# Triangular products of eight chunks in one run instead of two runs of four, in a decoder trunk with three token mixers

## The chip, the cores and the metric

The kernel runs on one core of a Trainium2 chip. The metric is the device time of one execution in microseconds; before the change its median over three runs is 2262.69 us (2262.41 to 2262.93).

The names of the engines in the profile: PE is TensorE (matmuls), PEld its weight loads, DVE is VectorE, ACT is ScalarE, POOL is GpSimd, and SP is SyncE, which issues the transfers.

## The reference, cut to what matters

The reference is a trunk of two layers over 1024 tokens of width 1024. Each layer takes an RMSNorm with a conditioned shift and scale, one wide input projection, three causal token mixers (pooling, retention, RWKV-7), a projection of each, gates, an output projection and the residual. The change lies in the RWKV-7 mixer, which has 8 heads of 64 channels and for each token:

```
def step(S, inp):
    r_t, w_t, k_t, v_t, a_t, b_t = inp
    sa = jnp.einsum('bhvk,bhk->bhv', S, a_t)
    S = (S * w_t[:, :, None, :] + sa[..., None] * b_t[:, :, None, :]
         + v_t[..., None] * k_t[:, :, None, :])
    return S, jnp.einsum('bhvk,bhk->bhv', S, r_t)
```

The kernel does this in 16 chunks of 64 tokens. Inside a chunk the recurrence turns into triangular matrices: products of the decayed keys and removal vectors (b, k) with the decayed receptances and key directions (r, a), of which a mask keeps the causal part. These are the triangular products.

## The kernel before, in words

Activations lie with channels on the 128 partitions and tokens along the free dimension, in two halves of 512. Nearly all of TensorE's time goes into dense projections: 128x512 products, three for each tile of weights, since weights and activations are split into a high and a low part (acc in the profile).

The RWKV mixer runs over four pairs of heads in each of two layers (rwkv_task, L1296). For one pair: prepare(h) makes from k, r and v of half h the tiles AR and BK (both operands of the triangular products, 8 chunks to a half). scores(h) (L1402) follows: two times four transposes of BK (tile bt), then the triangular products, then a masking multiplication on VectorE that moves them from PSUM to the tile G, then bonus(h), a sum over a head by two products (tile bon). scores(0) runs side by side with prepare(1); scores(1) follows. After that come the value products (states, L1474, tile av), the inversion of the triangular matrices (invert, on VectorE in the double bank), the block products (blocks, L1493, 32x32), and the state loop over 16 chunks (L1527).

One triangular product multiplies 64 partitions (one head) by 128 columns on each side. The two heads of a pair lie on partitions 0 to 63 and 64 to 127, so the kernel issues them by turns, and the two run side by side on TensorE's two row halves. Each takes two matmul instructions in float32.

PSUM is split up so: three banks for the dense projections (psa, tag acc), two rotating banks shared by all small work (psm, function mx, L609: transposes, norms, scores, value products, retention, pooling), one double bank held for the whole kernel as a single tile "two" of 2 x 512 columns, of which cyt() (L619) hands out the halves by turns, and one bank "ch" (psc), which the state loop uses for the values inside a chunk and the state update (L1547). The lead-in uses "two" and "ch" too. In the triangular products before the change, head 0 writes a rotating bank and head 1 a half of "two".

The order of the work is set in two steps. First the program is recorded: nothing is issued, each operation goes into a list, with a clock of its own that decides which task comes next (a generator's yield is the time after which it wants to go on). Second, a planner (plan, L341) replays the list with estimated durations: at each step it takes the engine that is free first and, among its ready operations, the one with the smallest key; the key is the place in the list, and the RWKV lane gets 3000 places of advantage (BIAS, L121). An operation that needs a new tile waits until its tag has a free slot. "with nc.together()" (L270) makes several matmuls one operation, which is never broken up. Two rules of the planner touch the change: entering the 64-row form is priced at 250 ns and leaving at 200 (ENTER and LEAVE, L117), and an operation of 16 or more matmuls waits for up to four dense products since the last such one (SPELL, L476):

```
if len(o.calls) >= 16 and spell < SPELL:
    rest = [x for x in now if x.big]
    if rest:
        o = min(rest, key=lambda o: o.key)
```

All instructions are issued from one place, so every row of the profile has the line L548, and rows are told apart by their tiles.

Of the kernel before, what the change touches and what calls it, by code (L numbers as in the profile page):

```python
# [9 lines left out]
F32 = mybir.dt.float32  # L10
# [3 lines left out]
ALU = mybir.AluOpType  # L14
# [3 lines left out]
P = 128  # L18
# [4 lines left out]
HF = 512  # L23
# [538 lines left out]
def trunk_kernel(ctx, tc, xT, cvec, pos, vecs, consts, w_ada, w_all, pool_w, lora_w, out):  # L562
    nc = Log(tc.nc, tc)

    def pool(name, bufs, **kw):
        return PoolProxy(nc, ctx.enter_context(tc.tile_pool(name=name, bufs=bufs, **kw)), bufs, "")
# [12 lines left out]
    ps_c = pool("psc", 1, space=PSUM)  # L579
# [9 lines left out]
    def nm(s):  # L589
        uid[0] += 1  # L590
        return f"{s}_{uid[0]}"
# [17 lines left out]
    def mx(s):  # L609
        t = ps_m.tile([P, HF], F32, tag="mx", name=nm(s))  # L610
        if len(mxq) == 2:
            behind[t.name] = mxq.popleft()
        mxq.append(t.name)
        return t
# [4 lines left out]
    def cyt():  # L619
        turn[0] ^= 1  # L620
        return two[:, turn[0] * HF : (turn[0] + 1) * HF]
# [4 lines left out]
    def r8(s):  # L626
        return rp.tile([P, 2048], F32, tag="r8", name=nm(s))

    o = CST["bone"]
# [8 lines left out]
    def cs(k, n=None):  # L638
        o = CST[k]
        return cst[:, o : o + n] if n else cst[:, o : o + 1]  # L640
# [165 lines left out]
    hd = [dp.tile([8, 2, P, HF], F32, name=f"hd{l}") for l in range(L)]  # L806
# [28 lines left out]
    def settle():  # L835
        if seen[0] is None:
            return
        for j in range(seen[0], len(nc.ops)):
            o = nc.ops[j]
            e, ins, outs = o.eng, o.ins_, o.outs  # L840
            t = max([ready.get(x.tensor.name, 0.0) for x in ins] + [0.0])
            base = t if any(x.space == PSUM for x in ins) else clock[0]
            if e == "PE":
                t = clock[0] + 280
            elif e != "SP":
                c = cost(o)
                idle_at[e] = max(idle_at[e], base) + c
                t = max(t + c, idle_at[e]) + 80
                for x in ins:
                    if x.space == PSUM:  # L850
                        ready[x.tensor.name] = max(ready.get(x.tensor.name, 0.0), t)
            for x in outs:
                ready[x.tensor.name] = t
        seen[0] = len(nc.ops)

    def await_(out, *ins):
        names = [x.tensor.name for x in ins] + [behind.pop(out.tensor.name, "")]
        clock[0] = max(clock[0], *(ready.get(n, 0.0) for n in names))
# [16 lines left out]
    def wait(*aps, spare=0.0):  # L875
        settle()
        names = [x.tensor.name if hasattr(x, "tensor") else x.name for x in aps]
        t = max(ready.get(n, 0.0) for n in names) + spare
        if len(mxq) == 2:
            t = max(t, ready.get(mxq[0], 0.0) + 600)  # L880
        return max(0.0, t - clock[0])
# [8 lines left out]
    def until(t):  # L890
        return max(0.0, t - clock[0])
# [51 lines left out]
    def mmul(out, lhsT, rhs, start=True, stop=True, timed=False, **kw):  # L943
        n = rhs.free_size()
        fast = rhs.dtype == F32R
        settle()
        await_(out, *(() if timed else (lhsT, rhs)))
        m = lhsT.free_size()
        clock[0] += (n + 32) / 2.4 if fast else 2 * max(n, 1.6 * m - 92, m - 16) * 0.875
        return nc.tensor.matmul(out, lhsT=lhsT, rhs=rhs, start=start, stop=stop, **kw)  # L950

    def trans(out, in_, timed=False):
        settle()
        await_(out, *(() if timed else (in_,)))
        clock[0] += 109.0
        nc.tensor.transpose(out, in_, ident)
# [339 lines left out]
    def rwkv_task(l, hp, kT, rT, vp, lt):  # L1296
        lw = lora_load(l, hp)
        AR = r8("AR").rearrange("p (c j t) -> p c j t", j=2, t=CH)
        BK = r8("BK").rearrange("p (c j t) -> p c j t", j=2, t=CH)
        Gf = gtile("G")  # L1300
        G = Gf[:, 0 : 32 * P].rearrange("p (u n) -> p u n", n=P)
# [6 lines left out]
        rm = cs("rmask", P).unsqueeze(1).to_broadcast([P, 4, P])  # L1308
        jt = lambda t, rows, c: t[rows, c, :, :].rearrange("p j t -> p (j t)")
# [81 lines left out]
        def bonus(h):  # L1391
            yield wait(*rks[h], spare=500)
            ps = mx("bon")
            mmul(ps, bone, rks[h][0], start=True, stop=False)
            mmul(ps, bone, rks[h][1], start=False, stop=True)
            bv = t_ri("bv")
            nc.vector.scalar_tensor_tensor(bv, ps, 0.5, vp[h], op0=ALU.mult, op1=ALU.mult)
            bvs.append(bv)
# [3 lines left out]
        def scores(h):  # L1402
            yield max(until(whole[h] + 1000), wait(Z, spare=600))
            for q in range(2):
                ps = mx("bt")
                c0 = 8 * h + 4 * q
                n = min(4, 15 - c0)
                with nc.together():
                    for c in range(n):
                        trans(ps[:, c * P : (c + 1) * P], jt(BK, slice(0, P), c0 + c), timed=True)  # L1410
                nc.scalar.copy(BKt[:, c0 : c0 + n, :], ps[:, 0 : n * P].rearrange("p (c n) -> p c n", n=P))
                yield 1300
            for q in range(2):
                c0 = 8 * h + 4 * q
                gps = [mx("g"), cyt()]
                with nc.together():
                    for j in range(4):
                        for hd in range(2):
                            rows = slice(64 * hd, 64 * hd + 64)
                            mmul(gps[hd][:, j * P : (j + 1) * P], jt(BK, rows, c0 + j), jt(AR, rows, c0 + j), timed=True)  # L1420
                for hd in range(2):
                    u0 = 16 * hd + c0
                    nc.vector.tensor_tensor(
                        G[:, u0 : u0 + 4, :], gps[hd].rearrange("p (u n) -> p u n", n=P), rm, op=ALU.mult
                    )
                yield 2600
            yield from bonus(h)
        yield from prepare(0)
        yield from side(scores(0), prepare(1))
        nc.gpsimd.memset(Z[0:64, :, :], 0.0)  # L1430
        yield from scores(1)
        prog[(l, hp)] = 0
        MT = r8("MT")
# [93 lines left out]
        for c in range(16):  # L1527
# [19 lines left out]
            ch = ps_c.tile([P, HF], F32, tag="ch", name=nm("ch"))  # L1547
            for hd in range(2):
                cols = slice(64 * hd, 64 * hd + 64)
                u0 = (16 * hd + c) * P  # L1550
                n = 65
# [24 lines left out]
            o = (c % 8) // 2 * P  # L1576
            yout.append(nc.scalar.copy(y[64 * par : 64 * par + 64, o : o + P], cy[0:64, 0:P]).ins)
            yield wait(Sn)
            if c % 8 == 7:
                h = c // 8  # L1580
# [370 lines left out]
    for l in range(L):  # L1951
# [200 lines left out]
        for p, (ia, ib) in enumerate(pairs):  # L2152
# [9 lines left out]
            for it in (ia, ib):  # L2162
                for h in range(2 if it[0] == "wg" else 0):
                    o = (t_vp if h else t_cs)("wo")
# [51 lines left out]
        while wready[0][0][0] != "out":  # L2216
# [6 lines left out]
            elif it[0] == "gate":  # L2223
                n, d = it[1], it[2]
# [3 lines left out]
            else:  # L2228
                n, d0 = it[1], it[2]
# [3 lines left out]
                for d, h in [(d, h) for h in range(2) for d in (d0, d0 + 1)]:  # L2233
# [5 lines left out]
                    o = (d % 2) * T + h * HF  # L2239
# [182 lines left out]
```

## Time and profile before

| | |
|---|---|
| median of three runs | 2262.69 us (2262.41 to 2262.93) |
| the profiled execution | 2262.4 us |
| its span | 2260.6 us |
| TensorE's granted clock, mean | 0.997 |
| triangular products, matmul instructions into the rotating bank / the double bank | 256 / 256 |
| masking multiplications on VectorE | 64, some 0.68 us each |

The page of the profile gives busy times of the engines, the span in 40 slices, the chain of work that ended last, and groups of instructions. Further views answer for a part: groups by line and tile, the timeline (instructions in order, with "xN" for N merged ones, and in brackets the idle time before one with what ended it), and busy time by stretches. Of the names in the rows, g is the rotating bank's tile of triangular products, two is the double bank, ch the bank of the intra-chunk values, acc a dense projection, and G the masked result. Ends of matmuls are modelled, since they are pipelined; the distance between two starts is the better measure.

### The profile page before, as it was taken

How to read it: one execution, taken by the hardware profiler on the slowest of the kernel's cores; microseconds unless marked ns; L12 is line 12 of the kernel's file. 1: busy time of each engine (PE TensorE's matmuls, PEld its weight loads, DVE VectorE, ACT ScalarE, POOL GpSimd, SP SyncE). 2: the span in 40 equal slices, each digit the busy share in tenths (PEclk: the TensorE clock that was granted, in tenths of full speed). 3: DMA queues.
4: the chain of work that ended last, by engine and by line, in shares of the span. 5: the costliest groups of instructions: out<-in, count | busy, mean ns of one | idle time of the engine just before them, and what ended most of it. 6: DMA issues, size and time to landing. Idle time of an engine off the chain costs nothing.

```text
span 2260.6 us, 34881 instructions
## 1 busy us (share of the span) xinstructions
PE 2229.0 (99%) x12980; PEld 1865.3 (83%) x12980; DVE 1589.5 (70%) x2750; ACT 931.5 (41%) x1795; POOL 627.0 (28%) x564
## 2 busy tenths in 40 slices
PE   7999999999999999999999999999999999999998
PEld 6788888888888888888878888888888888888888
DVE  7996877958878765668667678587686744465854
ACT  5634434434344344323454343353443444442243
POOL 2223323323325233332122132333332500041311
PEclk9999999999999999999999999999999999999999
DMA  8222111112236664654541111111122533256442
GB/s 318 70 59 72 34 43 42 51 46 70 86 119 218 200 201 130 229 187 167 172 134 31 45 41 44 55 38 49 40 82 93 182 112 112 89 184 218 135 131 85
DMA packets 138906, 249.36 MB, mean 110 GB/s; under 512 B 15728, under 2 KB 20080, under 8 KB 138736
## 3 DMA queue, kind: packets, MB, share of 16 engines
q1 hardware_dynamic: 138736, 247.14, 34.1%
q8 instruction: 102, 1.67, 0.3%
q14 instruction: 68, 0.56, 0.1%
HBM read 187.57 MB, written 59.51 MB: 109 GB/s over the span
## 4 chain that ended last, share of the span: by engine, by line
PE 89%; DVE 7%; ACT 2%; issue 1%; DMA 1%; SPq 0%; DVEq 0%; ACTq 0%
PE acc L548 73%; PE two L548 3%; PE ch L548 2%; PE ro L548 1%; PE g L548 1%; PE av L548 1%; DVE two L548 1%; DVE tm L548 1%; DVE ksq L548 1%; PE rs L548 1%; DVE G L548 1%; PE rkv L548 1%; PE m L548 1%; PE bt L548 1%; PE lw L548 1%
## 5 line engine op out<-in xcount | busy, mean ns | idle before, releaser
L548 PE MATMUL acc<-hhi,wh 128*128 128x512 f32 x1488 | 597.1, 401 | 1.6 <-DVE vp L548 1.1
L548 PE MATMUL acc<-hhi,wl 128*128 128x512 f32 x1488 | 596.9, 401 | 0.0
L548 PE MATMUL acc<-hlo,wh 128*128 128x512 f32 x1488 | 596.3, 401 | 0.0
L548 POOL TENSOR_TENSOR wl<-wr,wh 128x512 fp32r<-128x512 f32 x171 | 228.4, 1335 | 585.8 <-ACT wh L548 440.5
L548 PEld LDWEIGHTS acc<-hhi,wh 128*128 128x128 f32 x1488 | 280.5, 189 | 50.8 <-DVE vp L548 1.5
L548 PEld LDWEIGHTS acc<-hhi,wl 128*128 128x128 f32 x1488 | 280.6, 189 | 48.7
L548 PEld LDWEIGHTS acc<-hlo,wh 128*128 128x128 f32 x1488 | 280.6, 189 | 47.3
L548 ACT CAST wh<-wr 128x512 fp32r<-128x512 f32 x242 | 149.3, 617 | 268.3 <-PE acc L548 215.5
L548 PE MATMUL acc<-T,wh 128*128 128x512 f32 x576 | 177.6, 389 | 0.0
L548 PEld LDWEIGHTS acc<-T,wh 128*128 128x128 f32 x576 | 108.1, 188 | 22.4
L548 DVE SCALAR_TENSOR_TENSOR S<-ch,pc,SP 64x64 f32<-64x64 f32 x224 | 63.3, 283 | 87.1 <-PE ch L548 84.3
L548 PE MATMUL acc<-T,wl 128*128 128x512 f32 x288 | 112.1, 389 | 0.0
L548 DVE TENSOR_TENSOR wl<-wsum,wh 128x512 fp32r<-128x512 f32 x63 | 45.3, 719 | 78.7 <-ACT wh L548 78.4
L548 ACT CAST wh<-wsum 128x512 fp32r<-128x512 f32 x96 | 59.5, 620 | 96.6 <-PE acc L548 92.9
L548 ACT COPY Z<-ch 64x128 f32<-64x128 f32 x128 | 33.0, 258 | 132.6 <-PE ch L548 132.0
L548 POOL TENSOR_TENSOR oz<-ol,oz 128x512 fp32r<-128x512 f32 x10 | 14.0, 1401 | 264.8 <-DVE wl L548 179.7
L548 DVE TENSOR_TENSOR tm<-MT,two 64x30 f32<-64x30 f32 (+14 forms) x240 | 76.3, 318 | 11.4 <-ACT two L548 4.6
L548 DVE TENSOR_TENSOR two<-two,tm 64x30 f32<-64x30 f32 (+14 forms) x240 | 78.9, 329 | 7.1
L548 PE MATMUL acc<-oy,wh 128*128 128x512 f32 x256 | 80.1, 394 | 0.0
L548 PE MATMUL acc<-oG,wh 128*128 128x512 f32 x256 | 79.0, 390 | 0.0
L548 PE MATMUL acc<-oz,wh 128*128 128x512 f32 x256 | 78.9, 389 | 0.0
L548 DVE TENSOR_TENSOR wl<-wraw,wh 128x512 fp32r<-128x512 f32 x48 | 33.7, 703 | 63.5 <-ACT wh L548 63.5
(332 smaller groups left out, 4863.5 us busy)
## 6 DMA issues: line engine op xcount, KB each, us to landing
wr<-in_w_all SPq DMA_DIRECT2D x268, 256.0 KB, 2.7
wraw<-in_w_all SPq DMA_DIRECT2D x96, 256.0 KB, 2.7
gd<-gsg SPq DMA_DIRECT2D x96, 256.0 KB, 2.0
gs<-gd SPq DMA_DIRECT2D x96, 256.0 KB, 3.8
wada<-in_w_ada SPq DMA_DIRECT2D x80, 256.0 KB, 2.9
ol<-od SPq DMA_DIRECT2D x48, 256.0 KB, 3.5
traw<-hd SPq DMA_DIRECT2D x32, 256.0 KB, 3.0
x<-in_xT SPq DMA_DIRECT2D x16, 256.0 KB, 5.2
```

The lines of the kernel that those rows point to most:

```text
L548: o.inst = f(*a, **k)
```

## The change

The two runs of four chunks become one run of eight. The first four chunks write a rotating bank (head 0) and one half of the double bank (head 1), as before. The other four write the bank "ch" and the other half of the double bank, where before they took a second rotating bank and the other half of the double bank. All 16 products are one operation of the planner. The four masking multiplications follow, two and two, with the same yields.

```
-            for q in range(2):
-                c0 = 8 * h + 4 * q
-                gps = [mx("g"), cyt()]
-                with nc.together():
-                    for j in range(4):
-                        for hd in range(2):
-                            rows = slice(64 * hd, 64 * hd + 64)
-                            mmul(gps[hd][:, j * P : (j + 1) * P], jt(BK, rows, c0 + j), jt(AR, rows, c0 + j), timed=True)
+            gps = [mx("g"), cyt(), ps_c.tile([P, HF], F32, tag="ch", name=nm("ch")), cyt()]
+            with nc.together():
+                for j in range(8):
+                    for hd in range(2):
+                        rows = slice(64 * hd, 64 * hd + 64)
+                        o = j % 4 * P
+                        mmul(
+                            gps[j // 4 * 2 + hd][:, o : o + P], jt(BK, rows, 8 * h + j), jt(AR, rows, 8 * h + j), timed=True
+                        )
+            for q in range(2):
                 for hd in range(2):
-                    u0 = 16 * hd + c0
+                    u0 = 16 * hd + 8 * h + 4 * q
                     nc.vector.tensor_tensor(
-                        G[:, u0 : u0 + 4, :], gps[hd].rearrange("p (u n) -> p u n", n=P), rm, op=ALU.mult
+                        G[:, u0 : u0 + 4, :], gps[2 * q + hd].rearrange("p (u n) -> p u n", n=P), rm, op=ALU.mult
                     )
                 yield 2600
```

## The prediction

> **What bounds the kernel now.** I read the page first, from the top: the span, the busy times, and the chain that ended last.
>
> ```profile
> span 2260.6 us, 34881 instructions
> PE 2229.0 (99%) x12980; PEld 1865.3 (83%) x12980; DVE 1589.5 (70%) x2750; ACT 931.5 (41%) x1795; POOL 627.0 (28%) x564
> PE 89%; DVE 7%; ACT 2%; issue 1%; DMA 1%; SPq 0%; DVEq 0%; ACTq 0%
> ```
>
> PE is busy for all but 31.6 us of the span, and the chain runs along PE for 89% of it. So latency on another engine is worth nothing by itself here: what counts is PE time that does no work. A busy share cannot show that, because overlapping matmuls count as busy even where their starts lie too far apart. I therefore went to the runs of the triangular products and read the distance between starts.
>
> Second view: busy time by stretch of the matmuls that write the rotating bank (tile g), one stretch around each of the 16 calls of scores. There is one call for each half of the sequence, eight pairs of heads in all. Four of the 16 rows and the sum; behind the stretch and its length stands PE's busy time with the count of instructions:
>
> ```profile
> 102.00:108.00 6.00, 2.31 (x16) 1.00 0.00 0
> 121.00:127.00 6.00, 2.40 (x16) 1.00 0.22 82
> 275.00:281.00 6.00, 2.05 (x16) 1.00 0.17 47
> 1659.00:1665.00 6.00, 2.05 (x16) 1.00 0.27 85
> sum 96.00, PE 35.71; mean PE 2.23
> ```
>
> Every stretch has the same 16 instructions, yet some need 2.05 us and others 2.31 or more. The 2.05 us rows are those in which the planner already puts the two runs of four chunks directly behind each other. There are seven of them (the first is at 275, the last at 1659), all in the second call for a head pair. The other nine are still split: all eight first calls, and the second call at 121. **So the change can only join nine runs, not sixteen.**
>
> **The change part by part. (a) One entry into and one exit from the 64-row form saved, nine times.** The timeline of PE around the split pair at 121, and around the joined pair at 275 (start, duration, engine, line, operation, output and inputs, shapes, count):
>
> ```profile
> 121.39 0.40 PE L548 MATMUL acc<-hlo,wh 128*128 128x512 f32 x1
> 121.72 0.37 PE L548 MATMUL g<-AR,BK 64*128 64x128 f32 x1
> ...
> 122.81 0.51 PE L548 MATMUL acc<-hhi,wl 128*128 128x512 f32 x1
> 123.15 0.40 PE L548 MATMUL acc<-hhi,wh 128*128 128x512 f32 x1
> 123.39 0.40 PE L548 MATMUL acc<-hlo,wh 128*128 128x512 f32 x1
> 123.62 0.40 PE L548 MATMUL acc<-hhi,wl 128*128 128x512 f32 x1
> 123.94 0.49 PE L548 MATMUL g<-AR,BK 64*128 64x128 f32 x2
> 124.25 0.37 PE L548 MATMUL two<-AR,BK 64*128 64x128 f32 x1
> ```
>
> ```profile
> 275.78 0.40 PE L548 MATMUL acc<-hhi,wh 128*128 128x512 f32 x1
> 276.10 0.37 PE L548 MATMUL g<-AR,BK 64*128 64x128 f32 x1
> ...
> 278.09 0.51 PE L548 MATMUL acc<-hlo,wh 128*128 128x512 f32 x1
> 278.43 0.40 PE L548 MATMUL bon<-rkh,bone 128*128 128x512 f32 x1
> ```
>
> Dense products follow each other every 0.23 us (123.15, 123.39, 123.62). I count from the last dense start before a run to the second full-width start after it and take off two such slots. The run of four chunks costs 123.15 - 121.39 - 0.46 = 1.30 us. Eight chunks joined cost 278.43 - 275.78 - 0.46 = 2.19 us. Two separate runs cost 2.60 us, so a join saves 0.41 us of PE.
>
> Five of the nine second runs are followed by the transposes of v, where leaving the form is cheaper:
>
> ```profile
> 1351.02 0.39 PE L548 MATMUL acc<-hlo,wh 128*128 128x512 f32 x1
> 1352.43 0.33 PE L548 MATMUL vt<-cst,vp 128*128 128x128 f32 x1
> 1352.60 0.38 PE L548 MATMUL vt<-cst,vp 128*128 128x128 f32 x2
> ```
>
> Here it is 1352.60 - 1351.02 = 1.58 us, less a dense slot of 0.23 and one transpose at its pace of 0.11 (the two merged into the last row take 0.38 together, one alone 0.27). That makes 1.24 us for the second run. Joined, the second half costs 2.19 - 1.30 = 0.89, so 0.35 us are saved. Sum of (a): 4 x 0.41 + 5 x 0.35 = **3.4 us**.
>
> The Trainium skill, TensorEngine Tiling (Array Packing), Key Properties, states that changing the tiling mode drains TensorE. Its page TensorE: Matmul & The Clock Gate, Single matmul latency, gives a fixed part of about 166 ns warm for a matmul that cannot hide its drain. Estimated from that page, two changes of mode cost 0.33 us and nine joins 3.0 us; the rows say 0.35 to 0.41, so the mechanism agrees and the size is nearly its own.
>
> **(b) The wait inside the second run goes.** In the row at 123.94 the second run starts, but its first product for the other head, into the double bank, starts 0.31 us later, at 124.25. Through that time PE is held: the queue is in order. On VectorE, and at the last split:
>
> ```profile
> 123.52 0.68 DVE L548 TENSOR_TENSOR G<-two,cst 128x512 f32<-128x512 f32 x1
> 1644.99 0.48 PE L548 MATMUL g<-AR,BK 64*128 64x128 f32 x2
> 1645.31 0.37 PE L548 MATMUL two<-AR,BK 64*128 64x128 f32 x1
> ```
>
> The first run's double-bank half is read until 123.52 + 0.68 = 124.20, and the held matmul starts 0.05 us behind that, although it writes the other half. The double bank is one tile, and the wait is set for the whole of it. Seven of the nine second runs are held so, by 0.09 to 0.42 us (0.31 at 124.25, 0.32 at 1645.31, the last), together **1.8 us**. In the joined run all products are issued before any of its own evictions, so nothing holds them: the run at 276.10 shows none of it.
>
> **(c) One rotating-bank tile fewer per call.** The second quarter of the products goes to the intra-chunk bank instead. After the joined pair at 276:
>
> ```profile
> 277.30 0.69 DVE L548 TENSOR_TENSOR G<-g,cst 128x512 f32<-128x512 f32 x1 [1.85 <-PE g L548]
> 278.84 0.68 DVE L548 TENSOR_TENSOR G<-g,cst 128x512 f32<-128x512 f32 x1
> 279.44 0.68 DVE L548 TENSOR_TENSOR G<-two,cst 128x512 f32<-128x512 f32 x1
> 279.13 0.39 PE L548 MATMUL acc<-hhi,wh 128*128 128x512 f32 x1
> 279.67 0.72 PE L548 MATMUL av<-Z,G 128*65 128x64 f32 x9
> ```
>
> The value products (av) start 0.54 us behind a dense product instead of 0.23, right behind the eviction that ends at 279.52. They write the rotating bank that this eviction frees, not what it produces: their chunks belong to the first call. That is 0.31 us, in four of the eight pairs (279.67 the first, the others at 1368, 1515 and 1663). With the new layout only the first eviction frees a rotating bank, which was done at 277.99, 1.5 us earlier, and the other bank is free from the start. So I take 4 x 0.31 = **1.2 us**. Nothing back would be the lower end.
>
> **(d) What is added.** The run now needs the intra-chunk bank and both halves of the double bank at once. Both were last used by the state loop of the head pair before:
>
> ```profile
> 386.87 0.40 PE L548 MATMUL ch<-xst,G 128*65 128x64 f32 x4
> 403.52 0.37 PE L548 MATMUL g<-AR,BK 64*128 64x128 f32 x1
> ```
>
> That loop ends 16 us before the next run (this is the narrowest of the seven), so no wait: zero. The planner lets an operation of 16 or more products wait until four dense ones have passed since the last such operation. The only ones before are the block products, which lie ahead of the state loop that has just been shown to be over; so this is zero too. The four evictions of one call stay four; their order on VectorE is free to change.
>
> Sum: 3.4 + 1.8 + 1.2 = 6.4 us. The profiled execution took 2262.4 us (span 2260.6), so 2256.0 for it. The median of the runs is 2262.69, 0.3 us above it, which gives **2256.3 us**. The time cannot be sharper than the planner: it fits the whole order anew around the change, and the stalls that its estimates miss move by up to about 2 us either way (all of PE's idle time together is 31.6 us).
>
> **The rivals.** *Banks and evictions give it back.* The four evictions follow a run at 0.60 us each (278.84, 279.44), 2.4 us, while the run itself takes 1.8 us. If VectorE now sets the pace, the next user of a rotating bank waits in place of the second run. In the first calls that would be the transposes of v, and the av wait stays. At the av price of 0.31 us that is 8 x 0.31 = 2.5 us lost and 1.2 not gained: 6.4 - 3.7 = 2.7 us faster, 2260.0 us. For it: VectorE is 70% busy and in these stages more. Against: the merged run fills its first bank halfway, so that bank is emptied while PE goes on (277.30, with the run lasting to 278.09). The Trainium skill, TensorEngine Tiling (Array Packing), PSUM Bottleneck, warns of just this, that packing speeds up TensorE but not the emptying of PSUM; the seven joined runs of this trace show it in the av wait alone.
>
> *Slower: the chain behind a first call becomes late.* With the run of eight chunks ahead of the norm products of the other half, those come 0.89 us later. If all four evictions also go ahead of them on VectorE, two more evictions of 0.60 us lie in the way: 2.1 us per head pair, 16.8 us over eight. Net it would be 6.4 - 16.8 = 10.4 us slower, 2273.1 us. It decides only where PE has no dense product left to fill with. Against it:
>
> ```profile
> 405.00:552.00 147.00, 146.92 (x1015) 123.02 (x1014) 109.99 (x220) 61.45 (x130) 45.88 (x46) 1.00 0.16 52
> ```
>
> From 405 to 552, a whole head pair, PE idles 0.08 us. The chain has cover, and the second evictions are recorded 2600 ns of the planner's clock behind the first, so they need not go ahead.
>
> *The change does less than it says*, in that the planner has joined most runs already: that is no rival but a row, and stands in the sum (nine, not sixteen). It cannot do nothing, since one grouped operation cannot be split.
>
> **How the numbers follow.** The forecast case (a + b and most of c) has 0.68. Its own range is 2253.5 to 2258.2: the sum less or plus the 2 to 3 us by which the order can shift. The case in which banks and evictions give it back has 0.26 and runs from 2258.2 to 2262.7. The late chain has 0.06. The range of 8 in 10 reaches from 2253.5 to 2261.0. It leaves out the late chain, the last part of the second case and a little below. No change is 0.2% here, 4.5 us, about what a measurement of this kernel can tell; so faster means below 2258.2. Faster 0.68, same 0.26, slower 0.06.
>
> **What would show it.** In the new profile: sixteen runs of 32 matmul instructions, none of 16; g tile stretches with half the instructions each; no start of a double-bank product more than 0.02 us behind its partner's; av directly on a dense product's 0.23 us slot; PE busy time down by about what the span loses. It is wrong if transposes of v or bonus products start more than 0.5 us behind a dense product, if the intra-chunk bank turns up as a reason for waiting, or if PE idles in the state loops.

## The result, and the profile after

The changed kernel takes 2255.75 us (median of six runs, 2254.5 to 2260.26) against 2262.83 us for the kernel before in the same measurement: a ratio of 0.9968 with a 95% interval of 0.9955 to 0.9981, 7.1 us faster. A second measurement on another occasion gave 2255.98 against 2261.82 us, 0.9976 (0.9967 to 0.9985). The forecast was 2256.3.

The page of the profiled execution (2256.61 us):

```profile
span 2254.8 us, 34865 instructions
PE 2224.4 (99%) x12980; PEld 1865.8 (83%) x12980; DVE 1590.2 (71%) x2753; ACT 931.2 (41%) x1795; POOL 628.3 (28%) x561
PE 90%; DVE 6%; ACT 2%; issue 1%; DMA 0%; POOL 0%; SPq 0%; DVEq 0%; POOLq 0%; ACTq 0%
```

The same 12980 matmul instructions are there, PE is busy for 4.6 us less, and the span is 5.8 us shorter. This execution had a slower start: the first triangular run begins at 104.36 us instead of 103.08, with the same order of PE's work up to there. From that point to the end (2260.6 - 103.1 against 2254.8 - 104.4) the change gained 7.1 us.

Busy time by stretch, here of the matmuls into the double bank (tile two), one stretch around each of the 16 calls; two of the rows and the sum:

```profile
102.00:108.00 6.00, 2.05 (x16) 1.00 0.00 0
121.00:127.00 6.00, 2.05 (x16) 1.00 0.28 89
sum 96.00, PE 32.77; mean PE 2.05
```

All sixteen calls now need 2.05 us; none is split. The timeline of PE around the call that was split at 121, here from 122:

```profile
122.67 0.40 PE L548 MATMUL acc<-hlo,wh 128*128 128x512 f32 x1
123.00 0.37 PE L548 MATMUL g<-AR,BK 64*128 64x128 f32 x1
123.00 0.37 PE L548 MATMUL two<-AR,BK 64*128 64x128 f32 x1
...
124.98 0.51 PE L548 MATMUL acc<-hhi,wl 128*128 128x512 f32 x1
125.32 0.40 PE L548 MATMUL acc<-hhi,wh 128*128 128x512 f32 x1
```

From the dense start at 122.67 to the second one behind the run, at 125.32, it is 2.65 us, as long as the joined run of before. The first product into the double bank starts with its partner (123.00 and 123.00), not 0.31 us behind. And VectorE and PE behind the second call of the second head pair:

```profile
275.62 0.69 DVE L548 TENSOR_TENSOR G<-g,cst 128x512 f32<-128x512 f32 x1 [1.47 <-PE g L548]
276.53 0.69 DVE L548 TENSOR_TENSOR G<-two,cst 128x512 f32<-128x512 f32 x1 [0.22 <-PE two L548]
277.14 0.68 DVE L548 TENSOR_TENSOR G<-ch,cst 128x512 f32<-128x512 f32 x1
277.74 0.68 DVE L548 TENSOR_TENSOR G<-two,cst 128x512 f32<-128x512 f32 x1
```

```profile
277.22 0.39 PE L548 MATMUL acc<-hlo,wh 128*128 128x512 f32 x1
277.45 1.10 PE L548 MATMUL av<-Z,G 128*65 128x64 f32 x16
```

The value products start 0.23 us behind a dense start, while the eviction of the intra-chunk bank is still going on. The wait of 0.31 us is gone.

### The profile page after: what moved, and what is told of

Read it like the earlier page. It is cut to its first block, busy times and chain, and to the rows that moved or that the text cites. A ratio compares the mean times of both kernels' runs of the same rounds, so it can differ in the third digit from the quotient of the medians.

```text
span 2254.8 us, 34865 instructions
## 1 busy us (share of the span) xinstructions
PE 2224.4 (99%) x12980; PEld 1865.8 (83%) x12980; DVE 1590.2 (71%) x2753; ACT 931.2 (41%) x1795; POOL 628.3 (28%) x561
## 4 chain that ended last, share of the span: by engine, by line
PE 90%; DVE 6%; ACT 2%; issue 1%; DMA 0%; POOL 0%; SPq 0%; DVEq 0%; POOLq 0%; ACTq 0%
PE acc L548 74%; PE two L548 3%; PE ch L548 3%; PE av L548 1%; PE ro L548 1%; DVE two L548 1%; DVE tm L548 1%; PE g L548 1%; PE rs L548 1%; DVE ksq L548 1%; PE bt L548 1%; PE lw L548 1%; PE rkv L548 1%; DVE G L548 0%; PE m L548 0%
## 5 line engine op out<-in xcount | busy, mean ns | idle before, releaser
L548 DVE TENSOR_TENSOR tm<-MT,two 64x30 f32<-64x30 f32 (+14 forms) x240 | 76.3, 318 | 13.1 <-ACT two L548 6.3
L548 ACT COPY y<-two 64x128 f32<-64x128 f32 x128 | 33.1, 258 | 108.5 <-PE two L548 106.9
```

The source lines that it names most:

```text
L548: o.inst = f(*a, **k)
```

## The experiments

The kernels were measured in several groups, on different chips, each together with the kernel before, whose median was 2261.82 to 2262.83 us. The ratios are to the kernel before in the same group; differences of times across groups are uncertain by about 1 us.

To compare the profiled executions I add up by how much the starts of PE's instructions lie further apart than at the usual pace (228 ns for a dense product of 512 columns, 110 for 128 columns, 56 for an instruction of a triangular product). There are three sums. *Cost of the 64-row form*: around each run of triangular products, from the last start before it to the second behind it; it holds entries, exits and held products. *Stalls*: other starts over 110 ns late before which PE sat idle. *Halved clock*: the distances inside a spell in which the granted clock was 0.5; in brackets how long these spells last together. The last two are counted from 102.5 us (about the first triangular run) to 2240 us. The sums are my count from the traces, good to some 0.5 us; what they leave out differs from the kernel before by 1.7 us at most. Times are medians; the changed kernel's is 2255.75 us.

| kernel | time, us | ratio to before (95%) | 64-row cost, us | stalls, us | halved clock, us |
|---|---|---|---|---|---|
| before | 2262.83 | 1 | 11.6 | 11.8 | 0 |
| changed | 2255.75 | 0.9968 (0.9955 to 0.9981) | 6.5 | 9.9 | 0 |
| join_mx | 2268.33 | 1.0029 (1.0018 to 1.0039) | 6.3 | 18.3 | 5.0 (10.2) |
| join_mx_reserve | 2264.03 | 1.0008 (0.9999 to 1.0017) | 6.6 | 12.6 | 4.6 (6.8) |
| bank_only | 2264.72 | 1.0010 (1.0000 to 1.0019) | 9.8 | 15.2 | 3.3 (6.8) |
| same_banks | 2261.47 | 0.9997 (0.9988 to 1.0006) | 12.6 | 9.6 | 1.6 (3.4) |
| extra_pair | 2271.36 | 1.0042 (1.0029 to 1.0054) | 12.2 | 13.1 | 3.2 (6.8) |
| before, pattern 1 / 2 | 2262.10 / 2264.69 | 0.9994 (0.9985 to 1.0004) / 1.0008 (0.9998 to 1.0017) | 11.4 / 11.6 | 10.9 / 13.6 | 1.6 (3.4) / 1.6 (3.4) |
| changed, pattern 1 / 2 | 2257.78 / 2254.78 | 0.9979 (0.9969 to 0.9989) / 0.9964 (0.9951 to 0.9977) | 6.4 / 6.5 | 12.0 / 9.4 | 0 / 0 |
| join_mx, pattern 2 | 2269.88 | 1.0035 (1.0021 to 1.0049) | 6.4 | 19.4 | 3.5 (6.8) |
| bank_only, pattern 2 | 2264.38 | 1.0004 (0.9995 to 1.0014) | 9.6 | 13.8 | 3.2 (6.8) |

**The price of the form: same_banks.** The second run of four writes the same two banks as the first, so all sixteen calls are split, and the planner knows of the wait.

```
-            for q in range(2):
+            gps = [mx("g"), cyt()]
+            cyt()
+            for q in range(2):
                 c0 = 8 * h + 4 * q
-                gps = [mx("g"), cyt()]
```

> Two operations of four chunks, of which the second writes the same two banks as the first and so has to wait for both evictions; no call of the sixteen can be joined, and the planner knows of the wait, so that nothing is held inside a run. Theory: against the changed kernel sixteen more entries and exits at 0.35 to 0.41 us, 5.6 to 6.6 us slower than the changed kernel, some 2262 us, that is within 1 us of the kernel before. Rival (a change of form costs little, the held runs and banks were the gain): within 2 us of the changed kernel, 2256 to 2258 us.

Measured: 2261.47 us, 5.7 us slower than the changed kernel (measured in another group). The 64-row cost went from 6.5 to 12.6 us, 0.38 for each of the sixteen additional runs. Busy time by stretch of tile g around one call:

```profile
402.00:406.00 4.00, 1.16 (x8) 1.00 0.27 85
406.00:411.00 5.00, 1.16 (x8) 1.00 0.00 0
```

Two runs of 1.16 us stand here for one of 2.05. The theory holds; the rival (2256 to 2258 us) falls.

**The price of a run of its own: extra_pair.** One more pair of products behind each call of the changed kernel, a run of its own.

```
                 yield 2600
+            with nc.together():
+                for hd in range(2):
+                    rows = slice(64 * hd, 64 * hd + 64)
+                    mmul(gps[2 + hd][:, 0:P], jt(BK, rows, 8 * h), jt(AR, rows, 8 * h), timed=True)
             yield from bonus(h)
```

> The changed kernel, in which each of the sixteen calls issues, behind its evictions, one more pair of triangular products (the fifth chunk's, a second time, with no reader). Each is a run of its own. Theory: an entry and an exit (0.41 us) and a pair at 0.11 us, sixteen times: 8.3 us slower than the changed kernel, some 2264 us. Rival (a change of form costs little): only the pairs' own 16 x 0.11 = 1.8 us, some 2257.5 us.

Measured: 2271.36 us, 15.6 us slower than the changed kernel, nearly twice what was expected. The timeline of PE shows the pair itself, and, much later, where more was lost:

```profile
110.07 0.39 PE L548 MATMUL acc<-hlo,wh 128*128 128x512 f32 x1
110.39 0.37 PE L548 MATMUL ch<-AR,BK 64*128 64x128 f32 x1
...
110.81 0.50 PE L548 MATMUL acc<-hhi,wl 128*128 128x512 f32 x1
111.14 0.39 PE L548 MATMUL acc<-hhi,wh 128*128 128x512 f32 x1
...
1802.00 0.50 PE L548 MATMUL acc<-hhi,wh 128*128 128x512 f32 x1 [0.71 <-ACT acc L548]
...
1806.01 0.73 PE L548 MATMUL acc<-T,wh 128*128 128x512 f32 x2 [2.62 <-ACT wh L548]
```

From 110.07 to 111.14 it is 1.07 us; less two dense slots, 0.61 us for a pair alone. My expectation took 0.11 us for the pair's own time, but a product is two instructions, so it is 0.22, and 0.39 for the form. Sixteen times (somewhat less where value products follow), that is the 64-row cost, 5.8 us above that of the changed kernel, plus 16 x 0.22 = 3.5, together 9.3 us. The other 6 us are accounted for by the entry of the second layer's product stage (waits of 0.71, 2.62 and 0.58 us against one of 0.50 in the changed kernel) and by two spells of halved clock (3.2 us), one behind the wait of 2.62 us and one at the change of layer (last section). The rival, 2257.5 us, falls.

**The join without the bank: join_mx.**

```
-            gps = [mx("g"), cyt(), ps_c.tile([P, HF], F32, tag="ch", name=nm("ch")), cyt()]
+            gps = [mx("g"), cyt(), mx("g"), cyt()]
```

> The eight chunks are one run, as in the change, but the second quarter goes to a second rotating bank, as before the change, and not to the intra-chunk bank. All sixteen calls issue 32 instructions in one run. Theory (entries and exits 3.4 us, held second runs 1.8 us, bank 1.2 us): 5.2 us faster than the kernel before, about 2257.5 us, and the four waits of av behind the second eviction of the rotating bank (0.31 us each) are still there. Rival (the freed rotating bank is what pays, the join is not): within 2 us of the kernel before.

Measured: 2268.33 us, 6.4 us **slower** than the kernel before. Neither theory foresaw it. The joins are there and pay what they should (64-row cost 6.3 us, 5.3 less than before); but the stalls rose by 6.5 us, and in two spells PE ran at half its clock, which cost another 5.0 us. Two rows of PE's timeline, and busy time by stretch within the two spells (the fourth column is the granted clock):

```profile
134.46 0.37 PE L548 MATMUL g<-AR,BK 64*128 64x128 f32 x1
481.36 0.18 PE L548 MATMUL two<-G,MT 32*32 32x32 f32 x1 [1.21 <-DVE G L548]
```

```profile
483.40:490.10 6.70, 6.70 (x54) 0.50 0.07 24
1186.60:1189.90 3.30, 3.30 (x9) 0.50 0.00 0
```

The first head pair's second call starts at 134.46 us; in the changed kernel it starts at 123.00. A run that needs both rotating banks at once must find both free, while every other lane is content with one. Its chain then runs late: the state loop of the third head pair starts some 20 us later than in the changed kernel. PE covers most of such lateness with dense products, but not all: at 481.36 the block products of that pair sit 1.21 us waiting for VectorE. The first spell of halved clock starts 2 us behind that wait, the second behind the wait at the change of layer, which the kernel before has too, without a spell. Without both spells this kernel would still be no faster than the one before, since by these sums the stalls alone take back what the joins save; that the late chains caused the spells is not shown.

The other half of the expectation fell too. The four waits of av, which were to stay because the second rotating bank stays, are gone: in all eight pairs the value products start 0.23 to 0.24 us behind a dense start. The first of the four, for which the kernel before shows 0.54:

```profile
293.51 0.40 PE L548 MATMUL acc<-hlo,wh 128*128 128x512 f32 x1
293.75 1.10 PE L548 MATMUL av<-Z,G 128*65 128x64 f32 x16
```

The prediction's first rival (banks give it back) has its point here: not in the change, but in the change without its third bank, and there it is the joined run itself that waits for banks, not the user behind it.

**The same, with freed banks kept for the run: join_mx_reserve.**

```
                     ok = len(slots[tag]) >= len(mine) and mine[0] == next(x for x in q if seen[x].lane == o.lane)
+                    if o.lane != "rwkv":
+                        first = next((x for x in q if seen[x].lane == "rwkv"), None)
+                        ok = ok and not any(p is seen.get(first) and len(p.calls) == 16 for p in parked.get(tag, ()))
```

> The join with two rotating banks, as in join_mx, which took 6 us more than the kernel before. In addition the planner keeps freed rotating banks for a run of eight chunks that is ready and stands first in its lane: other lanes get none until it has its two. In the recorded order fourteen of the sixteen runs move forward or stay, eight of them to within some 35 matmuls of their place in the changed kernel; the second call of the first head pair stays about as late as in join_mx. Theory (join_mx lost by waiting for two free rotating banks at once, so that the chains of layer 0 ran late and PE ran out of other work): 4 to 8 us faster than join_mx, 2260 to 2264 us, with the waits of PE around 690 to 715 us mostly gone. Rival (the two banks, held together, starve the other lanes, and that is the loss): as slow as join_mx or slower.

Measured: 2264.03 us, 4.3 us faster than join_mx and no faster than the kernel before (ratio 1.0008, 0.9999 to 1.0017). The second state loop ends 2 us later than before the change instead of 14, and the stalls fell from 18.3 to 12.6 us, so the waiting for two banks did cause most of the lateness. But the half of the expectation that spoke of the waits around 690 to 715 us fell. PE's timeline:

```profile
692.64 0.50 PE L551 MATMUL acc<-hhi,wh 128*128 128x512 f32 x1 [2.16 <-ACT wh L551]
```

A wait of 2.16 us stands there, longer than any in join_mx at that place. Late chains are not what decides this entry. A spell of halved clock follows that wait (694.63 to 701.46 us), and another wait of 1.64 us reaches into it; together these cost 4.6 us. That leaves this kernel level with the one before, although it has the joins.

**The bank without the join: bank_only.**

```
-                gps = [mx("g"), cyt()]
+                gps = [ps_c.tile([P, HF], F32, tag="ch", name=nm("ch")) if q else mx("g"), cyt()]
```

> Two operations of four chunks stay, as before the change, but the second one's head 0 writes the intra-chunk bank. The recorded order has nine split calls out of sixteen, as many as before the change. Theory: only the bank term, 1.2 us faster than the kernel before, about 2261.5 us; the waits of av are gone, the held second runs stay. Rival (the bank pays): 5 us faster or more, as much as the whole change.

Measured: 2264.72 us, 1.0010 (1.0000 to 1.0019): no faster than before, so neither the theory's 2261.5 us nor the rival's 5 us. The 64-row cost fell by 1.8 us, since the held second runs, which the theory expected to stay, are mostly gone; but two new waits of av and transposes (0.4 us each) came up, some 4.4 us were lost to waits and halved clock at the entry of the second layer's product stage, and 1.6 to halved clock at the change of layer.

**Is it the order? Patterns 1 and 2.** The planner's keys of all lanes but the most urgent were moved by up to 20 places either way, in the kernel before and in the changed one.

```
-SEED = 0
-SHAKE = 0
+SEED = 1
+SHAKE = 40
```

(SEED = 2 for pattern 2.)

> The kernel before with another order of the work outside the RWKV lane: the planner's keys of the other lanes are moved by up to 20 places either way, by a fixed pattern (1). Nine calls are split, as before. This shows how far the order alone moves the time. Theory: the order moves it by 2 to 3 us either way, 2260 to 2266 us. Rival (the gain of the change is luck of the order): by 6 us or more.

> The changed kernel under the same pattern (1). Theory: 5 to 8 us below the kernel before under the same pattern, since the gain comes with the nine joins. Rival (luck of the order): no nearer to 6.4 us below it than to nothing.

> The kernel before, keys moved by another pattern (2). Nine calls are split. Theory: within 3 us of the kernel before. Rival: off by 6 us or more.

> The changed kernel under pattern (2). Theory: 5 to 8 us below the kernel before under pattern (2). Rival: no nearer to 6.4 us below it than to nothing.

Measured: 2262.10 and 2257.78 us under pattern 1, 4.3 us apart; 2264.69 and 2254.78 under pattern 2, 9.9 apart. With the unshaken 7.1 the mean is 7.1. Against 2262.28 us in the same group the kernel before moved by 0.2 down and 2.4 up, the changed one by 2.0 up and 1.0 down. The changed kernel is faster under every order, with the same fall of the 64-row cost (5.0 and 5.1 us); what varies is the stalls (1.1 us more under pattern 1, 4.2 less under pattern 2) and the clock: in the profiled executions the kernel before lost 1.6 us to one halved spell under each pattern, the changed one none. Under pattern 1 the gap lies just outside the expected 5 to 8 us on the low side, under pattern 2 on the high side: the order is worth some 3 us either way on the difference.

**The two halves under another order: join_mx and bank_only with pattern 2.**

> join_mx (one run of eight chunks, two rotating banks) under pattern (2). Theory (needing two free rotating banks at once makes the calls late, whatever the order): again no faster than the kernel before under that pattern, 2264 to 2271 us. Rival (the loss of join_mx was the order alone): as fast as the joins make it, 2257 to 2260 us.

> bank_only (two operations of four chunks, the second one's head 0 in the intra-chunk bank) under pattern (2) of the planner's keys. Under that pattern the kernel before took 2264.7 us and the changed one 2254.8 us. Theory (the loss of bank_only against the kernel before was the order at the entry of the product stage, not the bank): between the two, 2259 to 2264 us. Rival (the bank alone costs time): slower than the kernel before under that pattern, over 2265 us.

Measured: 2269.88 us for the join alone, again 5.2 us above the kernel before under that pattern; 2264.38 us for the bank alone, equal to it and just above its expected 2259 to 2264. So the loss of join_mx does not hang on the order, and the bank alone brought nothing under either order. Its share is not measured free of the rest, though: both times bank_only lost 1.6 to 3.3 us more to halved clock than the kernel before.

**The change again: after_again.** The changed kernel, unedited.

> The changed kernel as it is, on the same chip as join_mx_reserve and the kernel before. Theory: 5 to 8 us faster than the kernel before, as in the first measurement. Rival (the first measurement was favoured by the chip): less than 4.5 us.

Measured: 2255.98 us, 5.8 us faster than the kernel before.

## Why the prediction was right, point by point

**Nine runs, not sixteen.** Right: nine calls were split, and all of them are joined now.

**(a) and (b), 3.4 + 1.8 = 5.2 us.** The 64-row cost fell from 11.6 to 6.5 us, 5.2 before rounding. The size is confirmed by same_banks (0.38 us for each additional run, predicted 0.35 to 0.41), under two other orders (5.0 and 5.1), and by the pair alone in extra_pair (0.39 for the form). The held second runs are gone in the joined ones, as the rows at 123.00 show.

**(c), 1.2 us.** The four waits of av are gone, as was forecast, and all stalls together fell from 11.8 to 9.9 us. The rest of that fall is a different set of waits and no more than the order moves: under pattern 1 the stalls rose by 1.1 us instead. That the total came out close to the forecast 6.4 is therefore in part luck; firm are the 5.2. And no run ties the four waits to the freed bank, for they are gone in join_mx too, where the second rotating bank is still taken. The step was also wrong in kind. It put the third bank down as a small gain of its own, to be added to that of the join. The experiments show that the two do not add up: the join alone loses 5 to 6 us (part of it to halved clock), the bank alone brought nothing, both together gain 7. The intra-chunk bank is what lets the run ask for one rotating bank only, and so be joined without waiting. The prediction named the sum rightly and would have given 5.2 us for join_mx.

**(d), nothing.** Right: the intra-chunk bank is no reason of any wait of PE in a triangular run. The waits of PE in the changed kernel, by who waited for whom, show what came instead:

```profile
PE two L548 <- DVE G L548: 0.6, 1, 0.6
PE acc L548 <- POOL wl L548: 0.5, 1, 0.5
```

The first is one run of block products, the second the entry of the second layer's product stage; neither stood in the list before.

**The rivals.** Evictions did not take the pace: the transposes of v behind the first calls and the bonus products behind all sixteen start 0.20 to 0.24 us behind the row before, far from the 0.5 that was named as the sign. The slower rival (a late chain behind the first call) did not come true in the change, but join_mx shows its mechanism and its price: there the state loops start 11 to 27 us later than in the changed kernel, and the stalls are 8.4 us higher. So PE's cover is large but not complete (the 7632 dense products, at 0.228 us each, are some 77% of the span, not nearly all of it), which the view of one head pair (0.08 us idle) could not show.

**What stays open.** How much is lost at the entry of the product stages (around 690 and 1790 us) goes from nothing to over 4 us with small moves in the order. There the last state loop, weight loads, sums of weights and splits come together, and I found no rule for which order does badly. Why a spell of halved clock follows some waits and not others is open as well.

## What to carry to other kernels

When a run of small products is joined to save changes of the array's form, count first how many are split in the trace, and then the banks that the joined run must hold at once: a bank from outside the shared pool can decide whether the join gains 7 us or loses 6. Where a wait is set for a tile of two banks as a whole, a reader of one half holds a writer of the other; issuing all writers ahead of the first reader removes it. In an order made by a planner, repeat a change under a few shaken orders before believing a part of it that is below the spread, here some 3 us. Read the granted clock beside the waits: in join_mx the spells of halved clock cost 5.0 us beside 6.5 us more of stalls.

## What the runs showed of the hardware that was not expected

The clock of PE can drop to half behind a wait of under 2 us. At the change of layer PE waits 1.4 to 2.1 us in each of these kernels (1.8 in the kernel before and the changed one), always for the same product of VectorE (r). In the kernel before the clock stayed whole; in bank_only it did not (busy time by stretch of PE, the fourth column the granted clock; first the kernel before, then bank_only):

```profile
1175.00:1179.00 4.00, 2.20 (x11) 1.00 0.48 178
```

```profile
1175.00:1179.00 4.00, 4.00 (x12) 0.57 0.00 0
```

In the second, eight dense products took 0.43 us each instead of 0.23, 1.6 us lost. The halved spells in the records last 3.41 us or a multiple of it, but for the one at the end of each execution. This agrees with the Trainium skill, TensorE: Matmul & The Clock Gate, Part 1, which tells of a free-running window of 3413 ns; but its table of advice sets the limit for harmless gaps at about 3 us, and here some 1.8 us was enough, in some kernels and not in others. The changed kernel's two profiled executions and those under both patterns had no such spell outside the start and the end. Over all fourteen profiled executions, the clock halved behind this wait in none of the three where it was 1.35 or 1.36 us, in four of the eight where it was 1.80 to 1.86 us (join_mx, bank_only, same_banks, extra_pair), and in all three where it was 2.13 us (the kernel before under both patterns, bank_only under pattern 2). Under the patterns the wait was 2.13 us in the kernel before and some 1.36 in the changed one, so that some 1.6 us of the gap there comes from this place. Whether the phase of a window decides among the eight was not tried.
